# Decoder layer on one core: the second half's projection spread over the whole of the second SSM and finished at its end

## The chip, the cores and the metric

The kernel runs on one core of a Trainium2 chip. The metric is the device time of one execution in microseconds (us); lower is better. Engines are named as the profile names them: PE (TensorE, matrix multiplication; PEld is its loading of weights), DVE (VectorE), ACT (ScalarE), POOL (GpSimd) and SP (SyncE, which here issues nearly all plain transfers). Each engine, and SP's queue, executes its own instructions strictly in the order in which the program lists them.

## The reference, cut to what matters

One layer of a hybrid decoder, on 1024 prompt tokens and 64 sample tokens. A projection of the normalised input gives u (for the SSM), q, k, v (for attention) and two gates; the SSM branch is a complex diagonal recurrence; attention is dilated and windowed; both branches are gated and merged, and a mixture of 16384 single-neuron experts (PEER) follows.

```python
xn = rmsnorm(x, g_mix)
u, q, k, v, ga, gb = split_projection(xn, w_in)
y_ssm, hT_re, hT_im = ssm_branch(u, h0_re, h0_im, ...)     # h[t] = a*h[t-1] + B u[t];  y = Re(C h) + D u
hs = jax.nn.gelu(y_ssm.reshape(B, S, SSM_WIDTH))
branch_a = (hs @ w_glu_a) * sigmoid(hs @ w_glu_b)
...                                                        # dilated attention of q, k, v -> attn
branch_b = attn @ w_attn_proj
x = x + (sigmoid(ga) * branch_a + sigmoid(gb) * branch_b) @ w_out
x = x + peer_ffn(rmsnorm(x, g_ffn), w_qp, sub_keys, u_tab, v_tab)
# peer_ffn: 8 heads x top 16 of 16384 experts per token:
#   act = gelu(xb . u_tab[eidx]);  out = sum(gate * act * v_tab[eidx])
```

## The kernel before, in words

The tokens are worked off in two halves: half 0 has 512 prompt tokens and the 64 samples, half 1 the other 512 prompt tokens. For each half the order is: projection, SSM (`ssm`), attention, GLU, `w_out`, PEER keys. Half 0 fetches its experts' rows one by one (`gather`, half 0 only); half 1 at the end multiplies with all experts (`dense`, from about 2650 us to the end).

Two streams of work run beside the main order, as Python generators: "ahead" is the projection of half 1 (`inputs`, `project_u`, `project`), and "gather" is the fetching of rows of `u_tab` and `v_tab`. The main order calls `tick(us)` with a rough time for what it has just issued; each stream is then advanced until it has given out as much as `us` times its own rate (`pace` sets a rate; for "ahead" it is `FILL[4]` = 1.5 in the second SSM, for "gather" `GO[2]` = 0.7). A row of "gather" counts as `RATE` = 1.9. `drain` advances a stream to its end, without giving anything to the other one.

```python
def tick(self, us):
    if self.inside:
        return
    for name in list(self.sides):
        s = self.sides[name]
        s[2] += us * s[1]
        while s[2] > 0 and name in self.sides:
            c = self.step(name)
            if name == "ahead":
                us += c
```

The list that comes out is then given to a scheduler, which lays the instructions of each engine in an order by a timeline of its own. So numbers in the ticks move instructions on every engine's list.

Names that matter below, with their lines. A *row* is an indirect DMA on POOL (L1558) that fetches 128 rows of `u_tab`, 128x1024 f32, 0.524 MB, into one of `RB` = 8 buffers; a *dot* is the DVE instruction (L1562) that multiplies such a block with the tokens, sums it, and frees the buffer. A *piece* of a weight matrix (0.524 MB) is loaded by SP (L132), cast on ACT to `wH` (L134) and its remainder made on DVE as `wL` (L136); one piece feeds 24 matmuls `mm<-xn.,w.` of 512 columns (two pieces 96 of 256 columns for v).

The second SSM, `ssm(1)`, has three parts. *Loads*: for eight groups q, `uk` and `P` are loaded (L677, L681), transposed and multiplied on PE, and written to the state `X` by ACT (L693). *Scan*: 23 steps on DVE of five instructions each (L711 to L715): 7 of 512 elements, 8 of 64, and 8 of 448, one for each q. *Output*: for each q, `M` and `Q` are loaded (L744, L746), PE does 16 matmuls of each (with `U`, L754, and with `X`), ACT applies Gelu into `Y` (L756), and SP stores `Y` to `hs_scr` (L763). `uk`, `ug`, `P`, `M`, `Q` and `Y` share six buffers, so two q are under way at most.

After the SSM comes attention: `attn_ahead(1)` loads the first q, k and v (L881 to L908), which needs the space that the projection's tiles held; DVE adds the mask (L931), and that writes into space that the SSM's tiles held, `Y` among them. Then DVE combines the three groups and PE transposes `hsn` for the GLU.

Of the kernel before, what the change touches and what calls it, by code (L numbers as in the profile page):

```python
# [37 lines left out]
RATES = (1.0, 1.3, 1.0, 1.0, 0.86, 1.0, 0.6)  # L38
RB = 8
GL = 20  # L40
GO = (2, 0, 0.7)
LEAD = 160

VT = (2, 3)
SSMT = (10.0, 0.0, 5.0)
NS = 2


# [19 lines left out]
class Prog:  # L68
# [231 lines left out]
    def phases(self, es):  # L300
# [21 lines left out]
        self.pace("ahead", FILL[4])  # L322
        self.pace("gather", GO[2])
        self.mark("ssm1")
# [332 lines left out]
    def ssm(self, h):  # L657
        tc, nc, a, s = self.tc, self.nc, self.a, self.scr[h]
        sm = h == 0
        nk = 64 + 8 * sm  # L660
        ng = 8 if h else 16
        v = nc.vector
        with tc.tile_pool(name=f"ssm{h}", bufs=1) as sp:
            U = sp.tile([128, 64, nk], F32, name="U")

            o = 8 * sm
            X = sp.tile([128, 65 + 2 * o, 64], F32, name="X")
            big = lambda nm: sp.tile([128, 128 * ng], F32, name=nm, tag="big", bufs=5 + h)
            if sm:
                nc.sync.dma_start(X[:, 0:8], a["h0"].rearrange("p (b g) -> p b g", b=8))  # L670
                v.memset(X[:, o], 0.0)
            else:
                v.tensor_copy(X[:, o], self.hfin)
            urow = s["u"].rearrange("(k t) c -> k t c", t=8)
            for q in range(64 // ng):
                uk = big("uk")[:nk].rearrange("k (s c) -> k s c", s=8)
                nc.sync.dma_start(uk, urow[:, :, q * 16 * ng:(q + 1) * 16 * ng])  # L677
                ug = big("ug")[:nk].rearrange("k (g s c) -> k g s c", g=ng, s=8)
                nc.scalar.copy(ug, uk[:, ::-1, :].rearrange("k s (g c) -> k g s c", g=ng))
                P = big("P").rearrange("p (g n) -> p g n", g=ng)  # L680
                nc.sync.dma_start(P, self.Pd[:, q * ng:q * ng + ng])  # L681
                for j0 in range(0, ng, 4):
                    ps = self.trt()
                    for j in range(4):
                        nc.tensor.transpose(ps[:, j * nk:(j + 1) * nk], ug[:, j0 + j].rearrange("k s c -> k (s c)"),
                                            self.ident[:nk, :nk])
                    g0 = q * ng + j0
                    nc.scalar.copy(U[:, g0:g0 + 4, :], ps[:, :4 * nk].rearrange("p (g k) -> p g k", g=4))
                    ps = self.trt()
                    pv = ps[:, :4 * nk].rearrange("p (g k) -> p g k", g=4)  # L690
                    for j in range(4):
                        self.mm(pv[:, j, :], P[:, j0 + j, :], U[:, g0 + j, :], start=True, stop=True)
                    nc.scalar.copy(X[:, o + 1:o + 65, g0:g0 + 4].rearrange("p k g -> p g k"), pv[:, :, nk - 64:])  # L693
                    if sm:
                        nc.scalar.copy(X[:, 73:81, g0:g0 + 4].rearrange("p k g -> p g k"), pv[:, :, 0:8])
                self.tick(SSMT[0])

            a8 = sp.tile([128, 8, 2, 64], F32, name="a8")
            nc.sync.dma_start(a8, self.a8)
            lo, hi = slice(0, 64), slice(64, 128)  # L700

            def step(c, p, a, sh):

                n = 64 * sh[1] if len(sh) == 3 else 64 if len(sh) == 2 else 448
                t1, t2 = (sp.tile([128, 512], F32, name="st", tag="st", bufs=2)[:, :n] for _ in range(2))
                if len(sh) == 3:
                    t1, t2 = (t.rearrange("p (x g) -> p x g", g=64) for t in (t1, t2))
                if len(sh) == 4:
                    t1, t2 = (t.rearrange("p (x y g) -> p x y g", x=8, g=8) for t in (t1, t2))
                w = lambda x: x.to_broadcast([x.shape[0]] + sh[1:])  # L710
                v.tensor_mul(t1, w(p), w(a[0]))  # L711
                v.tensor_mul(t2[lo], w(p[hi]), w(a[1][hi]))
                v.tensor_mul(t2[hi], w(p[lo]), w(a[1][lo]))
                v.tensor_add(c, c, t1)
                self.last = v.tensor_add(c, c, t2)  # L715

            if h:
                self.drain("ahead")
                self.es1.close()
                self.attn_ahead(1)  # L720

            xv = X[:, o + 1:o + 65].rearrange("p (j i) g -> p i j g", i=8)
            xb = X[:, o:o + 64].rearrange("p (j i) g -> p j i g", i=8)
            one = [a8[:, 0, x].unsqueeze(1) for x in range(2)]
            for i in range(1, 8):
                step(xv[:, i], xv[:, i - 1], one, [128, 8, 64])
                self.tick(SSMT[1])
            for j in range(8):
                step(X[:, o + 8 * j + 8], X[:, o + 8 * j], [a8[:, 7, x] for x in range(2)], [128, 64])
                self.tick(SSMT[1])  # L730
            for gs in range(0, 64, 8):
                g = slice(gs, gs + 8)
                step(xb[:, :, 1:8, g], xb[:, :, 0:1, g], [a8[:, None, 0:7, x, g] for x in range(2)], [128, 8, 7, 8])
                self.tick(SSMT[1])
            if not sm:
                nc.sync.dma_start(a["ssm_p"], X[:, 64])
            else:
                v.tensor_copy(self.hfin, X[:, 72])
                step(X[:, 73:81], X[:, 0:8], one, [128, 8, 64])
                nc.sync.dma_start(a["ssm_s"], X[:, 73:81])  # L740
            hrow = [self.scr[i]["hs"].rearrange("(k t) c -> k t c", t=8) for i in range(2)]
            for q in range(64 // ng):
                M = big("M").rearrange("p (g x) -> p g x", g=ng)
                nc.sync.dma_start(M, self.Mx[:, q * ng:q * ng + ng, :])  # L744
                Q = big("Q").rearrange("p (g x) -> p g x", g=ng)
                nc.sync.dma_start(Q, self.Qd[:, q * ng:q * ng + ng, :])  # L746
                Y = big("Y")[:nk].rearrange("k (t c) -> k t c", t=8)
                for j0 in range(0, ng, 4):
                    ps = self.mmt() if h else self.trt()
                    pv = ps[:nk].rearrange("k (g x) -> k g x", g=4)  # L750
                    for j in range(4):
                        gl = j0 + j
                        g = q * ng + gl
                        nc.tensor.matmul(pv[:, j, :], lhsT=U[:, g, :], rhs=M[:, gl, :], start=True, stop=False)  # L754
                        self.mm(pv[:, j, :], X[:, :o + 64, g], Q[:, gl, :], start=False, stop=True)
                    nc.scalar.activation(Y[:, :, j0 * 16:j0 * 16 + 64].rearrange("k t (g c) -> k g t c", g=4),  # L756
                                         pv.rearrange("k g (t c) -> k g t c", t=8), AF.Gelu_apprx_tanh)
                cols = slice(q * 16 * ng, (q + 1) * 16 * ng)
                if sm:
                    nc.sync.dma_start(hrow[1][0:8, :, cols], Y[0:8])  # L760
                    nc.sync.dma_start(hrow[0][:, :, cols], Y[8:72])
                else:
                    nc.sync.dma_start(hrow[1][8:72, :, cols], Y)  # L763
                self.tick(SSMT[2])


    def nat(self, x, g, i):
# [464 lines left out]
    def peer_keys(self, h):  # L1232
# [7 lines left out]
        with ExitStack() as es:  # L1240
# [15 lines left out]
            with tc.tile_pool(name=f"pk{h}", bufs=1, side="right") as kp, ExitStack() as eg:  # L1256
# [28 lines left out]
                for i in range(ntl):  # L1285
                    rows = 128 if i < 4 else 64
                    self.choose(kp, h, i, rows, sv[i], si[i], (lambda: self.early(da, x)) if h else None)
                    if h == 0:
                        self.tick(30.0)
                    if h == 0 and i == GO[0]:  # L1290
                        self.beside("gather", self.gather(), GO[1])
                    if h:
# [452 lines left out]
```

## Time and profile before

| | |
|---|---|
| median of 3 runs | 4047.9 us (4040.63 to 4048.96) |
| the profiled execution, its own time | 4032.86 us |
| its span from first to last instruction | 4031.1 us |
| share of the span in which each engine is busy | PE 93%, DVE 73%, ACT 36%, POOL 36% |
| mean granted TensorE clock | 0.961 |
| moved by DMA | 1112.83 MB, 276 GB/s over the span |

The profiled execution is one execution with 1.8 us outside its span. All times on the trace are counted from the span's start.

### The profile page before, as it was taken

How to read it: one execution, taken by the hardware profiler on the slowest of the kernel's cores; microseconds unless marked ns; L12 is line 12 of the kernel's file. 1: busy time of each engine (PE TensorE's matmuls, PEld its weight loads, DVE VectorE, ACT ScalarE, POOL GpSimd, SP SyncE). 2: the span in 40 equal slices, each digit the busy share in tenths (PEclk: the TensorE clock that was granted, in tenths of full speed). 3: DMA queues.
4: the chain of work that ended last, by engine and by line, in shares of the span. 5: the costliest groups of instructions: out<-in, count | busy, mean ns of one | idle time of the engine just before them, and what ended most of it. 6: DMA issues, size and time to landing. Idle time of an engine off the chain costs nothing.

```text
span 4031.1 us, 72558 instructions
## 1 busy us (share of the span) xinstructions
PE 3738.5 (93%) x27907; PEld 3380.1 (84%) x27907; DVE 2943.4 (73%) x6796; ACT 1433.1 (36%) x2756; POOL 1444.1 (36%) x1236
## 2 busy tenths in 40 slices
PE   8889989899989967799979999879999999999997
PEld 8789965589878755597859899769999999999997
DVE  8627233445985767866999977668767999889986
ACT  3232224323234316322216888812222222222222
POOL 1620000000004424445563544433346755545550
PEclk9999989899999978899989999989999999999999
DMA  5574579544369989799897899999989999988993
GB/s 166 158 236 154 194 252 343 181 131 163 99 200 318 321 299 306 264 345 346 300 322 262 294 345 337 339 344 332 329 307 338 362 336 331 323 308 306 324 316 111
DMA packets 448987, 1112.83 MB, mean 276 GB/s; under 512 B 44656, under 2 KB 189424, under 8 KB 443008
## 3 DMA queue, kind: packets, MB, share of 16 engines
q1 hardware_dynamic: 301184, 571.26, 41.8%
q0 software_dynamic: 147456, 536.94, 37.0%
q8 instruction: 219, 3.59, 0.4%
q14 instruction: 128, 1.05, 0.1%
HBM read 991.77 MB, written 124.27 MB: 277 GB/s over the span
## 4 chain that ended last, share of the span: by engine, by line
PE 54%; DVE 6%; DMA 6%; issue 2%; ACT 2%; POOL 0%; SPq 0%; DVEq 0%; ACTq 0%; POOLq 0%
PE mm L80 31%; PE tr L80 20%; PE va L1640 2%; DVE row L1562 2%; DMA row<-in_u_tab,ei 1%; DMA G_scr<-Gt 1%; DMA Q<-Q_scr 1%; DVE wL L136 1%; DMA row<-in_v_tab,eT 1%; DMA V<-v_scr 0%; ACT Gt L1397 0%; DMA kT<-k_scr 0%; ACT sm L936 0%; DVE rest L1306 0%; DMA hs_scr<-Y 0%
## 5 line engine op out<-in xcount | busy, mean ns | idle before, releaser
L1558 POOL DMA_INDIRECT row<-in_u_tab,ei x512 | 664.3, 1297 | 986.7 <-DVE row L1562 451.3
L134 ACT CAST wH<-wraw 128x1024 fp32r<-128x1024 f32 (+1 forms) x476 | 492.3, 1035 | 1245.5 <-PE mm L80 915.5
L136 DVE TENSOR_TENSOR wL<-wraw,wH 128x1024 fp32r<-128x1024 f32 (+1 forms) x476 | 577.7, 1214 | 377.7 <-ACT wH L134 365.0
L1562 DVE SCALAR_TENSOR_TENSOR row<-row,gxn 128x1024 f32<-128x1024 f32 x512 | 616.8, 1217 | 48.4 <-DMA row<-in_u_tab,ei 41.8
L80 PE MATMUL tr<-x2H,wH 128*128 128x288 f32 x2048 | 611.7, 299 | 6.4 <-ACT a L1408 4.6
L80 PE MATMUL tr<-x2L,wH 128*128 128x288 f32 x2048 | 609.3, 297 | 0.0
L80 PE MATMUL tr<-x2H,wL 128*128 128x288 f32 x2048 | 609.1, 297 | 0.0
L80 PE MATMUL mm<-WH,wH 128*128 128x288 f32 (+2 forms) x2048 | 474.0, 295 | 18.6 <-ACT WH L186 18.2
L80 PE MATMUL mm<-WL,wH 128*128 128x288 f32 (+2 forms) x2048 | 473.8, 295 | 0.4 <-DVE WL L187 0.4
L80 PE MATMUL mm<-WH,wL 128*128 128x288 f32 (+2 forms) x2048 | 468.1, 294 | 0.0
L1590 POOL DMA_INDIRECT row<-in_v_tab,ei x256 | 350.9, 1371 | 293.3 <-DVE x3v L1596 240.7
L1624 POOL DMA_INDIRECT row<-in_v_tab,eT x256 | 315.7, 1233 | 386.4 <-DVE row L1562 228.4
L80 PEld LDWEIGHTS tr<-x2H,wH 128*128 128x128 f32 x2048 | 385.1, 188 | 16.3 <-ACT a L1408 7.2
L80 PEld LDWEIGHTS tr<-x2L,wH 128*128 128x128 f32 x2048 | 385.1, 188 | 2.5 <-issue 2.5
L80 PEld LDWEIGHTS tr<-x2H,wL 128*128 128x128 f32 x2048 | 385.0, 188 | 2.5 <-issue 2.5
L80 PEld LDWEIGHTS mm<-WH,wH 128*128 128x128 f32 x2048 | 339.8, 188 | 27.3 <-ACT WH L186 19.9
L80 PEld LDWEIGHTS mm<-WL,wH 128*128 128x128 f32 x2048 | 342.0, 188 | 4.1 <-issue 2.5
L80 PEld LDWEIGHTS mm<-WH,wL 128*128 128x128 f32 x2048 | 339.1, 188 | 1.7 <-issue 1.7
L1596 DVE SCALAR_TENSOR_TENSOR x3v<-row,act,x3v 128x1024 f32<-128x1024 f32 x256 | 327.4, 1279 | 3.0 <-DMA x3v<-x_scr 0.7
L80 PE MATMUL mm<-xnH,wL 128*128 128x288 f32 (+1 forms) x960 | 319.9, 333 | 2.7 <-DVE wL L136 2.7
L80 PE MATMUL mm<-xnH,wH 128*128 128x288 f32 (+1 forms) x960 | 322.3, 336 | 0.0
L80 PE MATMUL mm<-xnL,wH 128*128 128x288 f32 (+1 forms) x960 | 319.2, 332 | 0.0
(392 smaller groups left out, 7760.8 us busy)
## 6 DMA issues: line engine op xcount, KB each, us to landing
wraw<-in_vT SPq DMA_DIRECT2D x132, 512.0 KB
wraw<-in_uT SPq DMA_DIRECT2D x128, 512.0 KB
G_scr<-Gt SPq DMA_DIRECT2D x18, 2048.0 KB
G<-G_scr SPq DMA_DIRECT2D x32, 1152.0 KB
cc<-in_kc SPq DMA_DIRECT2D x48, 512.0 KB
cc<-in_vc SPq DMA_DIRECT2D x48, 512.0 KB
wraw<-in_w_g SPq DMA_DIRECT2D x32, 512.0 KB
wraw<-in_w_qp SPq DMA_DIRECT2D x32, 512.0 KB
```

Of the source, the lines that this page charges most:

```text
L80: self.last = self.nc.tensor.matmul(out, lhsT=lhsT, rhs=rhs, **kw)
L134: nc.scalar.copy(h, raw)
L136: nc.vector.tensor_sub(l, raw, h.bitcast(F32))
L1558: self.after(nc.gpsimd.indirect_dma_start(out=row, out_offset=None, in_=a["u_tab"], in_offset=bass.IndirectOffsetOnAxis(ap=ei[:, k:k + 1], ...
L1562: self.after(v.scalar_tensor_tensor(row, row, 1.0, xn, op0=ALU.mult, op1=ALU.mult, accum_out=act[:, k:k + 1]))
L1590: self.after(nc.gpsimd.indirect_dma_start(out=row, out_offset=None, in_=a["v_tab"], in_offset=bass.IndirectOffsetOnAxis(ap=ei[:, k:k + 1], ...
L1596: self.after(v.scalar_tensor_tensor(x3, row, self.gw[i][:, k:k + 1], x3, op0=ALU.mult, op1=ALU.add))
L1624: self.after(nc.gpsimd.indirect_dma_start(out=row, out_offset=None, in_=a["v_tab"], in_offset=bass.IndirectOffsetOnAxis(ap=eT[:, tk:tk + 1 ...
L1640: self.after(nc.tensor.matmul(va[0][c:c + 32, :], lhsT=self.strips[:, s, j, 31 - t - s:63 - t - s], rhs=rows[s * 2 + j][:, b * 512:(b + 1) ...
```

## The change

The projection of half 1 is no longer drained between the SSM's loads and its scan. The ticks of the second SSM are set apart from those of the first (`SSMT` now has a value for each half): 4.0 instead of 10.0 after each load group, 3.0 instead of 0 after each of the 23 scan steps, 5.0 as before after each output group; so both streams are advanced in the scan, too. From the output on, "gather" has the rate 0.4 instead of 0.7. What is left of the projection is drained after the output, and the first loads of attention are issued there.

```diff
-GO = (2, 0, 0.7)
+GO = (2, 0, 0.7, 0.4)
...
-SSMT = (10.0, 0.0, 5.0)
+SSMT = ((10.0, 4.0), (0.0, 3.0), (5.0, 5.0))
...
-                self.tick(SSMT[0])
+                self.tick(SSMT[0][h])
...
-            if h:
-                self.drain("ahead")
-                self.es1.close()
-                self.attn_ahead(1)
...
-                self.tick(SSMT[1])
+                self.tick(SSMT[1][h])
...
+            if h:
+                self.pace("gather", GO[3])
...
-                self.tick(SSMT[2])
+                self.tick(SSMT[2][h])
+        if h:
+            self.drain("ahead")
+            self.es1.close()
+            self.attn_ahead(1)
```

The lists of all engines are the same up to the second SSM's loads, with the same number of instructions in all. What stands where on DVE, in the scan, before (L1562 is a dot, L136 a piece of weights, L711 to L715 one scan step, here for two of the eight last steps):

```order
L715 TENSOR_TENSOR X<-X,st 128x8x7x8
L711 TENSOR_TENSOR st<-X,a_13984 128x448
L1562 SCALAR_TENSOR_TENSOR row,act<-row,gxn 128x1024 x2
L712 TENSOR_TENSOR st<-X,a_13984 64x448
L713 TENSOR_TENSOR st<-X,a_13984 64x448
L714 TENSOR_TENSOR X<-X,st 128x8x7x8
L715 TENSOR_TENSOR X<-X,st 128x8x7x8
L711 TENSOR_TENSOR st<-X,a_13984 128x448
```

And now, at the same place (a dot is L1564 here, since two lines were added):

```order
L715 TENSOR_TENSOR X<-X,st 128x8x7x8
L711 TENSOR_TENSOR st<-X,a_13376 128x448
L1564 SCALAR_TENSOR_TENSOR row,act<-row,gxn 128x1024 x2
L712 TENSOR_TENSOR st<-X,a_13376 64x448
L713 TENSOR_TENSOR st<-X,a_13376 64x448
L714 TENSOR_TENSOR X<-X,st 128x8x7x8
L136 TENSOR_TENSOR wL<-wraw,wH 128x1024
L1564 SCALAR_TENSOR_TENSOR row,act<-row,gxn 128x1024 x2
L715 TENSOR_TENSOR X<-X,st 128x8x7x8
L711 TENSOR_TENSOR st<-X,a_13376 128x448
L1564 SCALAR_TENSOR_TENSOR row,act<-row,gxn 128x1024
L136 TENSOR_TENSOR wL<-wraw,wH 128x1024
```

A scan step now has two to four dots and a piece of weights between its five instructions where it had none to two dots.

On DVE at the end of the scan, before (L931 is attention's first mask):

```order
L715 TENSOR_TENSOR X<-X,st 128x8x7x8
L1562 SCALAR_TENSOR_TENSOR row,act<-row,gxn 128x1024 x14
L931 ISA sm,stat<-mm,mask_69 128x256
```

And now (L933 is that mask's line now):

```order
L715 TENSOR_TENSOR X<-X,st 128x8x7x8
L1564 SCALAR_TENSOR_TENSOR row,act<-row,gxn 128x1024 x2
L136 TENSOR_TENSOR wL<-wraw,wH 128x1024
L1564 SCALAR_TENSOR_TENSOR row,act<-row,gxn 128x1024 x5
L136 TENSOR_TENSOR wL<-wraw,wH 128x1024
L1564 SCALAR_TENSOR_TENSOR row,act<-row,gxn 128x1024 x3
L136 TENSOR_TENSOR wL<-wraw,wH 128x512
L1564 SCALAR_TENSOR_TENSOR row,act<-row,gxn 128x1024 x12
L815 MEMSET stat 128x384 x2
L1564 SCALAR_TENSOR_TENSOR row,act<-row,gxn 128x1024 x6
L933 ISA sm,stat<-mm,mask_69 128x256
```

28 dots and three pieces of weights of the GLU stand between the scan and attention, where 14 dots stood.

On SP, at the output's second group of M and Q, before:

```order
L621 DMA sg_scr_140<-qo 128x512
L744 DMA M<-Mx_scr 128x1024
L746 DMA Q<-Q_scr 128x1024
L881 DMA q<-q_scr_137 128x1024
L888 DMA V<-v_scr_139 128x4x256
L897 DMA kT<-k_scr_138 128x2x512
L907 DMA V<-v_scr_133 128x256
L908 DMA kT<-k_scr_132 128x2x128
L763 DMA hs_scr_141<-Y 512x1x128
```

And now:

```order
L742 DMA M<-Mx_scr 128x1024
L744 DMA Q<-Q_scr 128x1024
L621 DMA sg_scr_140<-qo 128x512
L132 DMA wraw<-in_w_g 128x1024
L761 DMA hs_scr_141<-Y 512x1x128
L621 DMA sg_scr_140<-qo 128x512
L132 DMA wraw<-in_w_g 128x1024
L132 DMA wraw<-in_w_b 128x1024
L621 DMA sg_scr_140<-qo 128x512
L742 DMA M<-Mx_scr 128x1024
```

The loads of attention have left this place (they now stand after the sixth group's M and Q), and the last pieces of the projection's weights stand between the groups instead.

## Rows read from the trace of the kernel before

**Rows 1.** The page's head: span and number of instructions.

```profile
span 4031.1 us, 72558 instructions
```

**Rows 2.** Windows: stretch, length, busy us of PE, PEld, DVE, ACT, POOL, clock, DMA share, GB/s.

```profile
1200.00:1240.00 40.00, 33.78 (x165) 27.26 (x164) 10.79 (x15) 19.94 (x29) 4.60 (x3) 0.91 0.79 224
1240.00:1363.00 123.00, 118.08 (x682) 100.54 (x681) 73.23 (x109) 45.80 (x70) 60.99 (x47) 1.00 0.97 349
1363.00:1465.00 102.00, 80.52 (x361) 64.19 (x360) 98.96 (x178) 26.46 (x36) 32.82 (x25) 0.90 0.88 307
1468.00:1500.00 32.00, 19.56 (x115) 18.25 (x113) 12.86 (x22) 4.73 (x8) 17.02 (x13) 0.71 0.97 357
1465.00:1515.00 50.00, 34.94 (x208) 32.34 (x208) 16.04 (x29) 7.10 (x12) 18.98 (x14) 0.74 0.79 279
1515.00:1640.00 125.00, 98.63 (x893) 68.21 (x893) 94.20 (x324) 88.09 (x277) 60.64 (x48) 0.87 0.89 291
1640.00:1680.00 40.00, 21.87 (x74) 12.66 (x75) 37.75 (x75) 6.14 (x14) 17.32 (x15) 0.74 0.82 288
2700.00:4000.00 1300.00, 1299.58 (x9823) 1272.07 (x9822) 1103.05 (x1595) 349.94 (x490) 641.45 (x484) 1.00 0.88 315
```

**Rows 3.** The chain that ended last, end of the loads: start, us, what.

```profile
1339.87 9.80 PE mm L80 x42
...
1363.48 0.69 DVE st L711
```

**Rows 4.** DVE's groups by shape, 1363 to 1465 us: busy us, mean ns, idle before.

```profile
L1562 DVE SCALAR_TENSOR_TENSOR row<-row,gxn 128x1024 f32<-128x1024 f32 x24 | 28.7, 1218 | 0.1
L136 DVE TENSOR_TENSOR wL<-wraw,wH 128x1024 fp32r<-128x1024 f32 x13 | 15.8, 1219 | 0.1
L714 DVE TENSOR_TENSOR X<-X,st 128x448 f32<-128x448 f32 x8 | 5.0, 624 | 0.2
...
L714 DVE TENSOR_TENSOR X<-X,st 128x512 f32<-128x512 f32 x7 | 4.8, 686 | 0.0
...
L714 DVE TENSOR_TENSOR X<-X,st 128x64 f32<-128x64 f32 x8 | 1.8, 225 | 0.2
```

**Rows 5.** DVE's timeline, end of the scan to attention's first mask.

```profile
1463.69 0.62 DVE L715 TENSOR_TENSOR X<-X,st 128x448 f32<-128x448 f32 x1
...
1514.82 0.42 DVE L931 CUSTOM_DVE_ANT_0 sm<-mm,mask 128x256 f32<-128x256 f32 x1 [29.44 <-DMA hs_scr<-Y]
```

**Rows 6.** The chain that ended last, in the output: start, us, what.

```profile
1454.15 10.64 DMA Q<-Q_scr
1464.93 0.66 PE mm L80 x2
...
1472.60 8.57 DMA Q<-Q_scr
1481.31 0.66 PE mm L80 x2
...
1511.26 3.10 DMA hs_scr<-Y
```

**Rows 7.** Who waited for whom, 1228 to 1363 us: total us, times, longest.

```profile
POOL row L1558 <- DVE row L1562: 149.3, 17, 89.4
```

**Rows 8.** The same, 1465 to 1520 us.

```profile
POOL row L1558 <- DVE stat L933: 31.1, 1, 31.1
...
DVE row L1562 <- DMA row<-in_u_tab,ei: 4.5, 3, 3.4
```

**Rows 9.** Windows of line L1558 alone: stretch, length, POOL busy us (rows issued), clock, DMA.

```profile
1228.00:1363.00 135.00, 65.03 (x50) 1.00 0.95 340
1363.00:1410.00 47.00, 25.20 (x19) 1.00 0.91 310
...
1465.00:1515.00 50.00, 18.98 (x14) 0.74 0.79 279
```

**Rows 10.** DVE's groups by shape, 1640 to 1680 us.

```profile
L1562 DVE SCALAR_TENSOR_TENSOR row<-row,gxn 128x1024 f32<-128x1024 f32 x19 | 22.9, 1214 | 0.0
```

## What is expected, and how it is worked out

> **What bounds the kernel now.** I began with the windows. From 2700 to 4000 us PE is busy for 1299.58 of 1300 us at full clock [rows 2]: there PE is the bound, nothing before it is caught up later, and whatever the second SSM gains or loses arrives at the end of the span undiminished. The change acts between 1200 and 1680 us, and there the bound changes hands. In the loads, 1240 to 1363 us, PE is busy 118 of 123 us and DMA's share is 0.97 [rows 2]; PE works mostly on the projection. The scan, 1363 to 1465 us, is DVE's: 98.96 of 102 us [rows 2]. In the output, 1465 to 1515 us, nobody is busy: PE 34.94 of 50 us at a clock of 0.74 (between the levels 1.2 and 2.4 GHz), DVE 16.04 [rows 2]. The chain shows why: a Q load of 10.64 us, matmuls at 1464.93, another Q load, matmuls at 1481.31, and so on to the last store of `Y` at 1511.26 [rows 6]. Six buffers let two groups be under way, so loads come in bursts of two. DVE stands 29.44 us and begins attention at 1514.82, when that last store has landed [rows 5]: the mask writes where `Y` was. After attention, 1640 to 1680 us, DVE is busy 37.75 of 40 us [rows 2], and 19 dots, 22.9 us, are over half of that [rows 10].
>
> So the idle time is in the output; the projection's tail ran ahead of it, beside the scan.
>
> **The change, part by part.**
>
> *The loads end earlier.* I counted the lists. From the first transpose of `uk` to the last product with `P`, PE's list had 428 matmuls of the projection with 512 columns, and has 152; the 192 of 256 columns, and all 128 of the SSM are as before. A projection matmul takes 9.80 us / 42 = 0.233 us [rows 3]; 276 x 0.233 = 64 us, and 16 transposes of `kn` less give 1 or 2 more. The scan then starts at 1363.5 [rows 3] - 65 = 1298 us. This holds if PE's stalls stay as they are; they were 6.2 + 4.9 us [rows 2], and closer loads can double them: 1290 to 1310.
>
> *The scan gets longer.* Its own work is 7 x 5 x 0.686 + 8 x 5 x 0.225 + 8 x 5 x 0.624 = 58 us [rows 4]. The list put 23 dots and 14 pieces of `wL` between its instructions, and puts 55 and 21. Dots follow each other at 1.145 us (the next instruction starts before the accumulator is read), pieces take 1.219 [rows 4]. Check on before: 58 + 26.3 + 17.1 = 101; measured 1363.5 to 1464.3 = 101 [rows 3, 5]. Now: + 32 x 1.145 + 7 x 1.219 = 45, so 146 us, and the scan ends at 1444 instead of 1464. No gain in DVE's work, only its start moved.
>
> *The output.* In the lists 48 of its 256 matmuls (three of eight groups) now stand among the projection's last ones, and PE has 442 of the projection's 512-column matmuls, 103 us, from scan's start to the first output group; DVE finishes the first group's step after 16 of its 23 steps, 34 dots and 13 pieces: 36 + 39 + 16 = 91 us. So PE does not wait there, and three groups' M and Q land under the projection, which ends near 1444 as well. After that five groups remain. Before, the seven groups after 1464 took until 1511, 6.6 us each [rows 6]; five take 33 us, the store 3.1 [rows 6], so 1481. The first loads of attention, which used to go out before 1452, now stand between the groups: two sets of 1.8 MB (q, V and kT of 0.52 each, and 0.13 each of the first half's V and kT), 10 us at the rate of 357 GB/s [rows 2]. By the engines attention starts at 1481 to 1491.
>
> *The bytes.* Attention also waits for the dots that stand ahead of its first mask: 106 instead of 88. At 1515 us all eight buffers were full as well (POOL waited 31.1 us for DVE [rows 8]), 96 rows; now 106 to 110 must have come, 10 to 14 more, 6.3 MB at 0.524. Moved from 1200 to 1515 us: 224 x 40 + 349 x 123 + 307 x 102 + 279 x 50 = 97.2 MB [rows 2]. With 6.3 more, and 9.0 of it by 1240 as before, 94.5 MB are left. At a share of 0.97 DMA moved 349 and 357 GB/s [rows 2], 360 and 368 at a full share; at 364, 94.5 MB take 260 us, until 1500. At 349 it is 1511.
>
> The Trainium skill bears on this (DMA: Bandwidth & Descriptors, sections Issuing engines are not separate DMA queues, and Where 436 GB/s comes from): transfers started from several engines share the same 16 DMA engines and gain only issue time, and between HBM and SBUF the memory's side, about 358 GB/s per core, binds. It speaks against this change, since POOL's rows and SP's M and Q then divide one rate. By that page's figure attention starts, as an estimate, near 1504, by the engines' sum alone at 1481 to 1491; the rows at a share of 0.97 agree with the page.
>
> I take 1500, the byte sum: -15 us, bounds -34 (1481) and -4 (1511).
>
> *Attention* gets 47 dots instead of 40: 7 x 1.22 = +8.5 us if DVE sets its pace, nothing if not. DVE is busy 94 of 125 us and DMA's share is 0.89 [rows 2]; I take +6. The boundary between the first two token tiles, where new tokens `gxn` are loaded and eight dots wait for them, moves from attention's end to its middle; I price it within that.
>
> *Combining.* Between attention's last mask and the GLU's first instruction stand 14 dots instead of 30. Sixteen less are 18 us at 1.145, but PE must still transpose `hsn` and `hs_scr` must be loaded, PE being busy 21.87 us there at a clock of 0.74 [rows 2]. I take -13, bounds -18 and -5.
>
> *Later.* From there to `dense` 186 dots instead of 188, and beside `dense` seven rows of `u_tab` and eight of `v_tab` fewer, where PE is the bound: 0. The rate 0.4 is in these counts. The drain's work is covered by the wait for M and Q; without that cover it would cost what stands after the third group, 28 matmuls, 6.5 us.
>
> Sum: -15 + 6 - 13 = -22. On the profiled execution, 4032.9 us (the span of 4031.1 [rows 1] and 1.8 around it), that is 4011; that execution was 15 us faster than the median 4047.9, below all three timed ones. On the median I forecast 4047.9 - 22 = 4026 us.
>
> **The rivals.**
>
> *Rows come too slowly: slower.* After the scan's start 83 dots stand ahead of attention; with eight rows in the buffers 75 must be fetched. Attention and combining together give 7 us back, so it breaks even at 1514.8 + 7 = 1522 us: 75 rows in 224 us, 0.335 a microsecond. Below that DVE, which keeps its order, stands in the scan before dots whose rows have not come, and the output waits behind it. Measured: 50 in 135 us (0.37), 19 in 47 (0.40), but 14 in 50 (0.28) in the output [rows 9]. At 0.28, 75 rows take 268 us: attention at 1566, +51 - 7 = +44, 4092 us; at 0.32, 4058. For it: DMA is at 0.97 while rows, M and Q come together [rows 2]. Against it: POOL stood 149.3 us for buffers that DVE had not freed, longer than any other wait there [rows 7], and DVE waited only 4.5 us for rows in the output [rows 8], so 0.28 was not transport's limit.
>
> *The time is given back: same.* The bytes pass at 349 GB/s (1511, -4), attention pays its 8.5 us in full, and combining gains only 5 because `hsn` binds: about 0, 4048. For it: shares near 0.9 all through [rows 2], DVE's dots being moved and not removed. Against it: the 29 us in which DVE stands [rows 5] are now filled.
>
> *The engines' sum holds: faster still.* DMA passes more than the 364 GB/s taken, attention starts at 1481 without paying: -34 + 0 - 18 = -52, 3996. This is the near end of the forecast's own range, not a case apart.
>
> **How the numbers follow.** No change that is smaller than 0.2% (8 us) can be told from none here. The forecast (faster by 8 to 52 us, 3996 to 4040) gets 0.66, nothing 0.18, slower 0.16. The predicted time is the forecast's, 4026. The range 4000 to 4052 leaves out the forecast's last 4 us and the larger part of the slow rival, about 2 in 10. Faster 0.66, same 0.18, slower 0.16.
>
> **What would show it.** In the new trace: the first scan step (L711) near 1298 and the last (L715) near 1444, DVE busy throughout; three Gelus of `Y` pairs before the projection's last matmul; the first mask near 1500, its wait far under 29 us and ended by a row or by the last store; DMA share from 1240 to 1500 near 0.97; combining shorter by about 13 us; `dense` of the same length. Waits of DVE for rows (L1564 on `row`) of 20 us or more in the scan would speak for the slow rival. I am wrong if the loads do not come earlier (PE stalling for `uk` and `P`), or if later stages lie otherwise by more than 10 us through the scheduler's new order, which I priced at nothing.

## The result, and the profile after

The changed kernel takes 4075.2 us (median of 4 runs, 4068.18 to 4081.91), the kernel before 4046.1 us beside it (4 runs): a ratio of 1.0073, 95% interval 1.0055 to 1.0091. It is 29 us slower, where 4026 us was forecast. The profiled execution took 4068.18 us, of which its span, against that of [rows 1]:

```profile
span 4066.5 us, 72554 instructions
```

The windows from the loads to the first mask; columns as in [rows 2].

```profile
1240.00:1295.00 55.00, 55.00 (x396) 50.27 (x395) 27.98 (x42) 24.57 (x42) 22.23 (x17) 1.00 0.96 328
...
1295.00:1446.00 151.00, 141.05 (x614) 112.41 (x613) 141.07 (x246) 44.14 (x56) 72.14 (x55) 0.95 0.92 327
1446.00:1520.00 74.00, 31.24 (x166) 26.87 (x165) 37.12 (x62) 8.37 (x14) 40.20 (x29) 0.72 1.01 384
1240.00:1520.00 280.00, 227.29 (x1173) 189.55 (x1172) 206.18 (x348) 77.08 (x111) 134.56 (x100) 0.90 0.95 342
...
1520.00:1534.00 14.00, 11.51 (x78) 10.20 (x77) 0.09 (x1) 2.37 (x4) 0.00 (x0) 0.87 0.21 45
```

In the third window neither PE nor DVE is busy for much more than half of the time, while the DMA engines are full. DVE's timeline shows the same stretch (start, us, instruction; in brackets the idle time before it and its end): the scan's first step, its last, the last dot ahead of attention, the first mask.

```profile
1294.61 0.69 DVE L711 TENSOR_TENSOR st<-X,a 128x512 f32<-128x512 f32 x1 [0.18 <-ACT X L693]
...
1445.70 0.62 DVE L715 TENSOR_TENSOR X<-X,st 128x448 f32<-128x448 f32 x1
...
1497.16 1.22 DVE L1564 SCALAR_TENSOR_TENSOR row<-row,gxn 128x1024 f32<-128x1024 f32 x1
...
1533.91 0.42 DVE L933 CUSTOM_DVE_ANT_0 sm<-mm,mask 128x256 f32<-128x256 f32 x1 [35.52 <-DMA hs_scr<-Y]
```

DVE still stands for the store of `Y`, 35.5 us instead of 29.4 [rows 5], and from 1533.9 instead of 1514.8 on. Who waited for whom, 1440 to 1535 us:

```profile
PE mm L752 <- DMA M<-Mx_scr: 38.4, 4, 17.7
DVE sm L933 <- DMA hs_scr<-Y: 35.5, 1, 35.5
...
DVE row L1564 <- DMA row<-in_u_tab,ei: 9.1, 12, 2.1
```

PE stands for `M`; DVE hardly for rows. SP's queue shows the longest of these waits, that for the seventh `M`:

```profile
1473.77 0.32 SPq L621 DMA_DIRECT2D sg_scr<-qo  x1
1474.19 0.38 SPq L742 DMA_DIRECT2D M<-Mx_scr  x1
1474.66 0.39 SPq L744 DMA_DIRECT2D Q<-Q_scr  x1
1490.62 0.32 SPq L883 DMA_DIRECT2D q<-q_scr  x1
...
1500.04 3.18 SPq L883 DMA_DIRECT2D q<-q_scr  x1
...
1508.59 0.44 SPq L910 DMA_DIRECT2D kT<-k_scr  x1
1511.16 0.33 SPq L742 DMA_DIRECT2D M<-Mx_scr  x1
```

Attention's first load stands until the projection's last store (1473.77) has landed, and ten loads go out before the next `M` is asked for. What the DMA engines did meanwhile, 1465 to 1500 us (packets, MB, share of the 16 engines; POOL's rows are the software queue, everything SP issues the hardware queue):

```profile
DMA packets 5213, 14.34 MB, mean 410 GB/s; under 512 B 482, under 2 KB 1594, under 8 KB 5209
...
q0 software_dynamic: 2500, 9.10, 64.2%
q1 hardware_dynamic: 2709, 5.20, 38.9%
```

Rows took 64% of them. The loss does not end there. The table has starts in us from two traces of each kernel (the second ones are the runs c_before and c_after below, from another job). Its first row is an instruction ahead of the second SSM's loads, the last on DVE's list (its 2240th) up to which all kernels of this document agree:

```profile
1218.45 1.23 DVE L136 TENSOR_TENSOR wL<-wraw,wH 128x1024 fp32r<-128x1024 f32 x1 [10.87 <-ACT wH L134]
```

Here it is from the kernel after. It starts at 1216.2 us in the first trace of the kernel before and between 1215.9 and 1226.0 in the other traces, so clock times of two traces differ by up to 10 us before the change can act. Where that matters, a time below is *counted from the common start*, which means that this instruction's start is taken off; in this count the scan's first step comes at 76.0 to 76.2 us in eleven of the twelve traces with the change and at 77.7 in c_after.

| | before | c_before | after | c_after |
|---|---|---|---|---|
| common start | 1216.2 | 1218.4 | 1218.5 | 1222.1 |
| last Gelu of `Y` | 1510.7 | 1513.2 | 1529.7 | 1534.5 |
| first mask | 1514.8 | 1517.4 | 1533.9 | 1538.7 |
| last mask | 1620.5 | 1618.1 | 1644.1 | 1646.6 |
| last product of the GLU | 1820.4 | 1823.8 | 1835.5 | 1838.3 |
| first product of the PEER keys | 1898.4 | 1905.5 | 1924.7 | 1926.1 |
| first mask, counted from the common start | 298.6 | 299.0 | 315.5 | 316.6 |
| last product of the GLU, so counted | 604.1 | 605.4 | 617.1 | 616.2 |
| span | 4031.1 | 4046.1 | 4066.5 | 4083.3 |
| from the GLU's last product to the end | 2210.7 | 2222.3 | 2230.9 | 2245.0 |

Counted from the common start, the first mask is 17 to 18 us late, and by the GLU's end 11 to 13 us are lost. Behind it 20 and 23 more are lost, in stages that the prediction priced at nothing. Of these, 6 to 8 us lie between `w_out` and the keys, where PE's timeline has this row in the kernel after, and nothing of the kind in the kernel before:

```profile
1914.32 3.64 PE L1642 MATMUL va<-row,strips 128*32 128x512 f32 x16 [5.79 <-DMA row<-in_v_tab,eT]
```

Products of the row stream with rows of `v_tab` now stand in PE's list between the norm's transposes, and PE waits for their row.

### The profile page after: what moved, and what is told of

It reads as the page before. It is cut to its first block, busy times and chain, and to the rows that moved or that the text cites. A ratio compares the mean times of both kernels' runs of the same rounds, so it can differ in the third digit from the quotient of the medians.

```text
span 4066.5 us, 72554 instructions
## 1 busy us (share of the span) xinstructions
PE 3745.4 (92%) x27907; PEld 3388.8 (83%) x27907; DVE 2943.3 (72%) x6796; ACT 1438.4 (35%) x2756; POOL 1416.7 (35%) x1236
## 5 line engine op out<-in xcount | busy, mean ns | idle before, releaser
L1560 POOL DMA_INDIRECT row<-in_u_tab,ei x512 | 630.0, 1231 | 945.1 <-DVE row L1564 415.5
L136 DVE TENSOR_TENSOR wL<-wraw,wH 128x1024 fp32r<-128x1024 f32 (+1 forms) x476 | 577.3, 1213 | 380.4 <-ACT wH L134 363.7
L1564 DVE SCALAR_TENSOR_TENSOR row<-row,gxn 128x1024 f32<-128x1024 f32 x512 | 619.4, 1220 | 62.6 <-DMA row<-in_u_tab,ei 39.5
L80 PEld LDWEIGHTS tr<-x2H,wH 128*128 128x128 f32 x2048 | 387.3, 189 | 23.8 <-ACT a L1410 12.4
```

Of the source, the lines that this page charges most:

```text
L80: self.last = self.nc.tensor.matmul(out, lhsT=lhsT, rhs=rhs, **kw)
L136: nc.vector.tensor_sub(l, raw, h.bitcast(F32))
L1560: self.after(nc.gpsimd.indirect_dma_start(out=row, out_offset=None, in_=a["u_tab"], in_offset=bass.IndirectOffsetOnAxis(ap=ei[:, k:k + 1], ...
L1564: self.after(v.scalar_tensor_tensor(row, row, 1.0, xn, op0=ALU.mult, op1=ALU.mult, accum_out=act[:, k:k + 1]))
```

## The experiments

Each ratio is taken against runs of the kernel before on the same chip, in the same job.

**Why attention starts late.** Four kernels, each the kernel after with an edit. The first puts attention's loads behind the last `Q` in SP's list (an ordering without a wait):

```diff
+def ld(self, dst, src):
+    inst = self.nc.sync.dma_start(dst, src)
+    if self.behind:
+        self.tc.add_manual_dep(inst.ins, self.lastq.ins.name, ...)
...
+            self.behind = True
             self.attn_ahead(1)
+            self.behind = False
```

> The kernel after, with attention's first loads (q, V, kT) given out behind the last load of Q on SP instead of ahead of the last two groups' M and Q; rows and ticks as in the kernel after. Theory S (SP's order): M and Q of the last two groups no longer stand 15.5 us for the projection's last store and 20 us while ten loads are issued; group six is asked for near 1492 instead of 1511 us, the first mask comes near 1516 instead of 1534, and the time is about 18 us under the kernel after. Theory B (bytes): the 16 DMA engines are full from 1440 to 1520 us anyway; only the 3.6 MB of attention's loads move behind, 9 us at 400 GB/s: first mask near 1525, and then attention's first product waits for them. Theory L (later lists): at most half of the loss lies here; from the end of the GLU to the end the kernel still loses about 20 us against the kernel before, whatever the first mask does, so the time stays over the kernel before.

Measured: ratio 1.0014 (1.0002 to 1.0026). The common start and the last Gelu in this trace:

```profile
1226.00 1.23 DVE L137 TENSOR_TENSOR wL<-wraw,wH 128x1024 fp32r<-128x1024 f32 x1 [11.10 <-PE tr L81]
...
1521.28 0.59 ACT L755 ACTIVATE Y<-mm 64x512 f32<-64x512 f32 x1 [0.89 <-PE mm L81]
```

Counted from the common start the last Gelu comes at 295.3 instead of 311.3, 16.0 us earlier (by the clock it is 8.5, since this trace began the second SSM 7.5 us later). That is nearer to theory S's 18 than to theory B's 9. The bytes explain 9 of them: from the scan's end to 5 us before the last Gelu 25.1 MB moved instead of 28.6, at 388 GB/s. The rest goes with the loads' place: SP asks for the seventh `M` at 1495.4 instead of 1511.2 us, 23 us earlier counted from the common start, and the last two groups' `M` no longer land together behind everything else. The first mask came at 1531.4, only 10 us earlier in this count, since the last store of `Y` now stood behind the ten loads (10.1 us from Gelu to mask instead of 4.2). The time fell by 24 us by the ratios, of which 11 lie before the GLU's end (1832.1).

```diff
-GO = (2, 0, 0.7, 0.4)
+GO = (2, 0, 0.7, 0.0)
```

> The kernel after with gather's rate 0.0 instead of 0.4 in the output: 14 dots fewer ahead of the first mask (92 instead of 106). Attention's loads still stand ahead of the last groups' M and Q, now of three. Theory S: the first mask stays within 8 us of 1534, since SP still stands for the projection's last store. Theory B: 14 rows are 7.3 MB, 18 us at 400 GB/s: first mask near 1516. Theory L: the phase of the row stream changes by 8 to 14 rows in the later stages, and the time from the end of the GLU to the end changes by 10 us or more either way.

Measured: 1.0022 (1.0009 to 1.0036); last Gelu 1517.1, first mask 1521.2, 17.8 us earlier counted from the common start (1223.5). Theory B's 18 is met, and theory S, which allowed 8, fails as it was put. But the run does not part the two: without the rows SP's loads were issued faster too, and the seventh `M` was asked for at 1497.9, 18 us earlier in this count.

```diff
             if h:
+                self.drain("ahead")
+                self.es1.close()
+                self.attn_ahead(1)
                 self.pace("gather", GO[3])
...
-        if h:
-            self.drain("ahead")
-            self.es1.close()
-            self.attn_ahead(1)
```

> The kernel after with the drain, the release of the projection's space and attention's loads put between the scan and the output instead of behind the output; the ticks in loads and scan stay, so the projection is spread beside the scan, and attention's loads stand ahead of five groups, as before the change. Theory S: an early block on SP is as bad or worse than a late one, unless the projection's last store has landed by then; SP's stand for that store shows before the third group's loads, first mask at 1525 to 1545. Theory B: nothing of the bytes changes except the order; first mask near 1530. If the first mask comes before 1515 it was the late place of attention's loads that cost the time.

Measured: 1.0091 (1.0068 to 1.0113); first mask 1541.5. With attention's loads ahead of the whole output it comes 5.5 us later still, counted from the common start, so putting them back to their old place is no cure.

The fourth has the edits of the first and the second.

> Both the first and the second edit: attention's loads behind the last Q, and gather's rate 0.0 in the output (91 dots ahead of the first mask). Theory S: first mask near 1510, little better than with the first edit alone. Theory B: 3.6 + 7.3 MB leave the way of M and Q, 27 us at 400 GB/s: first mask near 1505, which is where the prediction's sum by engines and bytes put it. Theory L: the time from the end of the GLU to the end is what decides between faster and slower than the kernel before; with a first mask at 1505 and a loss of 20 us later, the time is 4050 to 4060.

Measured: 1.0010 (0.9993 to 1.0027). Last Gelu 1504.0, 28.5 us earlier than in the kernel after counted from the common start (1221.3), where B gave 27 for 10.9 MB and S 24. The mask stands behind the held-up store again:

```profile
1514.12 0.42 DVE L941 CUSTOM_DVE_ANT_0 sm<-mm,mask 128x256 f32<-128x256 f32 x1 [30.64 <-DMA hs_scr<-Y]
```

So what passes ahead of the last `M` and `Q` sets the output's end: 3.6, 7.3 and 10.9 MB less gave 16.0, 17.8 and 28.5 us, where the bytes alone come to 9, 18 and 27 at 400 GB/s. For the rows bytes are enough; for attention's loads SP's order counts as well. No run takes away SP's stand and leaves the bytes, so its share is not shown by itself. In the last of these kernels the GLU ends at 596.9 in the same count, 7 to 9 us ahead of the kernel before, and its time is still not lower: what is gained by then is lost behind the GLU, where it takes 2236.5 us.

**Two traces more.** Both kernels unchanged.

> The kernel before, unchanged: a second trace of it, since the profiled execution of before was 15 us under the median. Theory N (spread of executions): the stages up to the first mask agree within 5 us with the first trace (1514.8), and the stretch from the end of the GLU to the end is 10 to 20 us longer than its 2211 us. Theory L (the changed kernel's later lists cost 20 us): that stretch is again 2211 us within 5, and an early stage is what was fast.

> The kernel after, unchanged: a second trace. Its first mask is again at 1534 within 5 us, and the end of the GLU at 1836 within 5 if the cause of the loss is in the order of the bytes. From the end of the GLU to the end it took 2231 us in the first trace; theory N: 2225 to 2245, as much as a typical execution of before plus at most 10; theory L: 15 us or more over that of before in the same job.

Measured: 4047.9 and 4085.0 us, one run each; the table above has their stages. Theory N holds for the size of the spread (the stretch behind the GLU is 12 and 14 us longer than in the first traces) and L for the difference: 20.2 us in one pair, 22.7 in the other.

**Rows put off.** The kernel after with gather's rate 0.0 in the scan, and the kernel after without ticks in the scan.

```diff
+            if h:
+                self.pace("gather", 0.0)
             for i in range(1, 8):
```

> The kernel after with gather's rate 0.0 in the scan (and 0.4 in the output, as there): the projection alone is spread beside the scan; 45 dots instead of 106 ahead of the first mask, 163 instead of 198 by the end of the GLU. Theory B (bytes): 61 rows are 32 MB, so the DMA engines no longer bind; the scan is 50 dots or 57 us shorter on DVE (end near 1390), the projection on PE ends near 1415 and the output behind it near 1460: first mask 1455 to 1480. Theory G (the rows are only put off): the rows that are missing come back at 1.22 us of DVE each between the top 16 and the dense stage, where DVE is busy 223 of 237 us; 25 rows against the kernel before are 30 us, so the time is within 15 us of the kernel before although attention starts 40 us earlier. If the rows find room beside the dense stage, where DVE is busy 1103 of 1300 us, the time falls by 20 us or more against the kernel before.

```diff
-SSMT = ((10.0, 4.0), (0.0, 3.0), (5.0, 5.0))
+SSMT = ((10.0, 4.0), (0.0, 0.0), (5.0, 5.0))
```

> The kernel after with 0.0 instead of 3.0 after each scan step: neither stream is advanced in the scan; the second SSM runs almost by itself, and what is left of the projection is drained behind it, so attention waits for the projection. 32 dots at the scan's end, 50 ahead of the first mask, 167 by the end of the GLU. Theory B: the scan ends near 1375, the output near 1420, and the rest of the projection, of which PE had 103 us from the scan's start on, bounds attention's start: near 1480. Theory G as for the other: time within 15 us of the kernel before; else 20 us or more under it.

Measured: 1.0062 (1.0041 to 1.0084) and 1.0123 (1.0099 to 1.0148). Theory B's first masks are missed in both. In the second the projection ended at 1516.3 and the first mask came at 1530.4, not near 1480. In the first the scan ended at 1379.3, but the first mask came at 1513.5, not 1455 to 1480: with the DMA engines free, PE was the bound, and the projection ended at 1456.9, with five output groups behind it. Windows of that kernel, 1380 to 1460 us and the last 50 us:

```profile
1380.00:1460.00 80.00, 80.00 (x402) 65.40 (x401) 26.69 (x33) 23.53 (x32) 12.11 (x9) 1.00 0.65 211
...
4025.00:4075.00 50.00, 3.50 (x31) 3.27 (x30) 42.70 (x118) 3.45 (x6) 18.07 (x14) 0.56 0.69 245
```

The GLU ended at 1801.0, 24 to 25 us before that of the kernel before counted from the common start (1221.0), and all of it was lost again: PE is busy 3.5 of the last 50 us, where DVE and POOL finish the rows that were put off. In the kernel before POOL issues no row in its last 100 us. Theory G's sign is right, its size is not: 24 us gained by the GLU's end and 25 lost in all make about 49 us for 25 rows, more than DVE's 1.22 us each. What makes them dearer was not taken apart.

**Why the later stages lose.** Gather's rates alone, in the kernel after in the GLU and in the kernel before in attention.

```diff
-RATES = (1.0, 1.3, 1.0, 1.0, 0.86, 1.0, 0.6)
+RATES = (1.0, 0.9, 1.0, 1.0, 0.86, 1.0, 0.6)
```

> The kernel after with gather's rate in the GLU 0.9 instead of 1.3: up to the GLU nothing changes, and from there on the row stream stands as in the kernel before (210 dots at the first top 16, 265 at the first product of gates, 346 at the dense stage, as there; the kernel after has 220, 274, 353). Theory P (phase of the row stream): the loss behind the GLU comes from where the row stream's products with v rows and its change of token tiles fall; the stretch from the GLU's last matmul to the end, 2231 and 2245 us in two traces of the kernel after and 2211 and 2222 in two of the kernel before, comes back to 2210 to 2225, and the time falls by about 20 us against the kernel after, to some 15 us over the kernel before. Rival (order in general): the schedule of those stages is different for some other reason, the stretch stays at 2230 to 2245 and the time within 8 us of the kernel after.

Measured: 1.0012 (0.9998 to 1.0026). First mask 1537.4, as in the kernel after counted from the common start (315.2 for 315.5). The GLU's end, 1833.3, is 6 us earlier in this count, with 37 dots instead of 44 between the last mask and it. The stretch behind it is 2213.5, in the forecast 2210 to 2225. The products of `v_tab` are gone from between the norm's transposes: `w_out`'s last product and the first of the keys in PE's timeline.

```profile
1898.67 0.28 PE L80 MATMUL mm<-wH,mixL 128*128 128x256 f32 x1
...
1909.25 0.61 PE L80 MATMUL mm<-x2H,wH 128*128 128x288 f32 x1
```

10.6 us, where the kernel after needs 17.3.

```diff
-RATES = (1.0, 1.3, 1.0, 1.0, 0.86, 1.0, 0.6)
+RATES = (1.3, 1.3, 1.0, 1.0, 0.86, 1.0, 0.6)
```

> The kernel before with gather's rate in attention 1.3 instead of 1.0: the second SSM is untouched, and the row stream stands at the GLU's end as in the kernel after (198 dots instead of 188, and 222 at the first top 16). Theory P: the first mask stays at 1515 to 1518 us, the stretch from the GLU's end to the end grows by 15 to 25 us against the kernel before, and the time is 15 to 25 us over it, with nothing of the change in it. Rival: the stretch does not grow, and rows done earlier take 10 dots, 12 us of DVE, off the later stages; the time is the same or lower.

Measured: 1.0062 (1.0045 to 1.0079), 25 us more without any edit to the SSM. But most of it lies elsewhere than forecast: counted from the common start the GLU's end moves from 604.1 and 605.4 to 618.2, as attention, with 51 dots instead of 40, takes 117.6 us instead of 105.7 and 100.7. The stretch behind it takes 2214.9, no more than in the kernel before, although products of `v_tab` stand between the transposes here too. This run tells that ten rows taken early are not free; in it theory P fails for the stretch.

```diff
-RATES = (1.0, 1.3, 1.0, 1.0, 0.86, 1.0, 0.6)
+RATES = (1.0, 1.3, 1.0, 1.0, 0.86, 1.3, 0.6)
```

> The kernel before with gather's rate in w_out 1.3 instead of 1.0: no list differs up to the end of the GLU, 188 dots there as before; then 212 instead of 210 at the first top 16, 269 instead of 265 at the product of gates, 350 instead of 346 at the dense stage, nearly as in the two kernels without rows in the output (213, 268, 349), whose stretch behind the GLU took 2236 us. Theory P: the first mask and the GLU's end stay (1515 to 1518, 1820 to 1824), the stretch takes 2225 to 2240 instead of 2211 to 2222, and the time is 8 to 25 us over the kernel before, from two to four rows standing elsewhere. Rival: two to four rows do nothing; the time is within 8 us, and the later loss of the kernel after comes from its early part in some other way.

Measured: 1.0011 (0.9998 to 1.0025). First mask 1522.5, 301.0 counted from the common start (2 us later than before); stretch 2224.4, just short of theory P's 2225 to 2240. By the time the rival holds: two to four rows do little.

**Versions to beat both.** The first is the kernel after with the edits of e5_both, the second set of attention's loads behind the last store of `Y`, and 1.2 as the GLU's rate. The second is the kernel before with gather's rate 0.0 in the output and 1.2 in attention. The last two have gather's rates 0.0 and 1.6, and 0.2 and 1.2, in scan and output of the kernel after, with the loads placed as in the first.

> The kernel after with everything mended that the runs so far put a price on: attention's first loads behind the last Q, the second ones behind the last store of Y, no rows given out in the output, and gather's rate in the GLU 1.2, so that the row stream stands from the GLU on as in the kernel before (211, 265, 346). Theories B and P together: last Gelu near 1504 as with both edits, the store now at once behind it, first mask near 1508; behind the GLU as the kernel before; time 5 to 12 us under the kernel before. If the spread projection is itself the loss, the first mask is not before 1514, and the time is at or over the kernel before.

> The kernel before with gather's rate 0.0 in the second SSM's output, and 1.2 instead of 1.0 in attention, so that the row stream stands from the GLU on as in the kernel before (188, 210, 265, 346). 74 dots instead of 88 ahead of the first mask: 7.3 MB less of rows beside M and Q. Theory B: the DMA engines are at 0.97 there, so M and Q come up to 18 us earlier, first mask 1500 to 1505; attention takes the dots back at 1.22 us each as far as DVE sets its pace (14 dots, 17 us at most); time 0 to 15 us under the kernel before. If rows are not what M and Q wait for, the first mask stays at 1515 and the time is 0 to 10 us over it.

> The projection is spread beside the scan as in the kernel after; gather's rate is 0.0 in the scan and 1.6 in the output, so 57 dots stand between the scan's end and the first mask instead of 28, and the row stream stands from the GLU on nearly as in the kernel before (187, 210, 265, 345); attention's loads stand behind the last Q. Theories B and P: with the projection alone in the scan, the DMA engines moved 211 GB/s from 1380 to 1460 us while PE was the bound there; against 400 GB/s that is room for 15 MB or 28 rows, and DVE is idle two thirds of it. Rows put there cost little: scan's end near 1380, projection's end near 1457, last Gelu 1500 to 1510, end of the GLU at 1805 to 1820, then 2211 to 2222 us: 4018 to 4042 us in all, faster than both kernels by 8 us or more against the kernel before. Rival: the 12 rows for which there is no room come beside the last groups' M and Q, last Gelu at 1515 to 1525, and the time is that of the kernel before within 8 us.

> As the one before it, with gather's rate 0.2 in the scan and 1.2 in the output: 15 more dots in the scan (43 at its end), 46 behind it, 89 ahead of the first mask, 188 at the end of the GLU, 212 at the top 16. Theory B: rows for which there is no room behind the scan find it in the scan (175 GB/s moved from 1300 to 1380 with the projection alone): last Gelu 1500 to 1510, as in the run before it or up to 10 us earlier. Theory P: with 212 and 266 instead of 210 and 265 the row stream stands off its place, and the stretch behind the GLU's end takes up to 2236 us instead of 2211 to 2222.

Measured, in this order: 1.0006 (0.9988 to 1.0023), 1.0016 (1.0004 to 1.0029), 1.0089 (1.0063 to 1.0115), 1.0055 (1.0031 to 1.0079). None beats the kernel before. In e9_all_mended the store is free again (last Gelu 1508.7, first mask 1512.8, 288.9 counted from the common start, 10 us ahead of the kernel before), but attention takes 119.7 us and the GLU ends at 1830.1, 606.2 in this count, 1 to 2 us behind it. Its dots are not the reason, as 45 stand there and the kernel after has 47 in 110.2 us; DVE waited in attention 23.8 us for products of PE, and 12.4 there. What held PE up was not followed. So the two repairs do not add up: 1.0010 (e5_both) and 1.0012 (e7_after_rephased) each for itself, 1.0006 together. In e10_before_fewer_rows the first mask comes at 1510.9, 288.1 and so 10 to 11 us earlier in this count, which is theory B's forecast; the GLU's end is at 605.7, where it was: the 14 dots come back. In e11_rows_behind_scan the room that PE's bound left was hardly used: 18 rows were issued from 1380 to 1460, and 33 from 1460 to 1515, beside the last `M` and `Q`, at a DMA share of 1.03; DVE was through with its dots only at 1525.9, and the mask came at 1532.8. The last Gelu was where the forecast had it, 1509.2; the time is missed by the forecast and by its rival. In e12_rows_spread the last Gelu comes as in e11_rows_behind_scan (292.8 and 293.3 counted from the common start), as forecast, and the first mask at 302.9 instead of 316.9; the stretch of 2224.8 us is inside its bound.

## Why the prediction was wrong

*The loads end earlier*: right; 1294.6 (second trace 1299.8) for 1298.

*The scan gets longer*: right; it ends at 1445.7 for 1444, 151 us for 146.

*The output*: this is the first step that failed, by 34 us (first mask 1533.9 for 1500; 2.2 of them lie ahead of the second SSM). By engines: the first output group came at 1411.2, where 1401 follows from my 103 us, and the projection's last product at 1457.2; that it ends "near 1444" had no sum of its own behind it, and PE was already busy 141 of 151 us in the scan. Behind it five groups took 72.5 us to the last Gelu, where I summed 33. That 33 rested on a miscount: the Gelus of `Y` in the kernel before show two groups done by 1450 and six, not seven, behind the scan, 7.8 us each, so five would have been 39. Attention's loads, 10 us in this sum, cost 16 (e1). By bytes: the sum was nearly right, 342 GB/s x 280 us = 95.8 MB by 1520 for 94.5 forecast, but the rate was 342 and not 364, with shares of 0.96 and 0.92 in the first two windows: 16 to 20 us. And I took the last bytes to be a row's, behind which attention starts at once. They were those of the last `M` and `Q`; behind them stand their products, Gelu and store, 14 us. e1, e2 and e5 show it: whatever passes later lets the output end earlier. SP's queue had no term in my sum: it stood for the projection's last store and then for ten issues, 36 us from the sixth `Q` to the seventh `M`, and e1 shows that this order costs more than the loads' bytes. The wait under 29 us that I named as a mark became 35.5.

The slow rival had the right sign and the wrong place. It has DVE stand in the scan for rows; DVE waited 9.1 us for rows in all, 2.1 at the longest, and 29 rows were issued in 74 us (0.39 a microsecond, above the 0.335 at which it breaks even). Rows came fast enough; it was `M` and `Q` that they, and attention's loads, displaced.

*Attention*: right; 110.2 us from first to last mask instead of 105.7, +4.5 (second traces +7) for +6.

*Combining*: right in size; from the last mask to the GLU's last product 191.5 us instead of 199.9, -8.4 (second traces -14), for -13.

*Later*: this is the second step that failed: +20 us for 0, through the mark that I had named last, later stages lying otherwise by more than 10 us. I had counted dots and not looked at where they stand in PE's list. That the row stream is what costs most of this in the kernel after is shown by e7_after_rephased: the same kernel up to attention's end, ten rows fewer at the first top 16, the stretch back at 2213.5 and the time 25 us lower by the ratios. Whether it is the number of rows or where the lists put them, this run does not tell. In all 17 traces the time from `w_out`'s last product to the first of the keys went with one thing: 9.7 to 11.1 us in the seven whose list has only transposes there (the kernel before twice, e7, e9, e10, e12, e13), 13.9 to 18.5 us in the ten with products of `v_tab` between them. These products were not moved by themselves, and they do not decide the whole stretch: e8 has them and took 2214.9 us, e12 and e13 have not and took 2224.8 and 2224.4; two traces of one kernel are 12 and 14 us apart. Two things stay open: the other 12 to 17 us of the loss, of which 12 and 14 lie between the first product of the keys and PE's last longer gap ahead of the dense stage; and why e1_loads_behind, with the row stream's counts of the kernel after, lost less behind the GLU (2225.8). Every one of these kernels has its later lists laid anew, and the stretch took 2211 to 2247 us in those that finish their rows in time.

The dense stage, last, is right: from the end of PE's last longer gap (2695.0, before 2656.3) to the end 1371.5 us, before 1374.8.

Parts of the loss and its sum in the profiled pair: +2.2 ahead of the second SSM, which is not the change's, +16.9 from there to the first mask, +4.5 in attention, -8.4 up to the GLU's end, +20.2 behind it: 35.4 us, the difference of the spans.

## What to carry to other kernels

A stream of row fetches that is hidden by count still takes its share of the transfers: when the loads that the main order waits for must pass beside it, price what moves ahead of the last needed byte, and the work behind that byte. Where a scheduler lays all lists anew, a moved tick is a change to every later stage; look in each waiting engine's list for products whose operand comes by DMA, and count how many rows are left at the end, where nothing hides them. To tell what an edit did inside a long trace, count from an instruction that both lists have ahead of it: here clock times alone made an effect of 16 us look like 8.5, which hid that the order on SP's queue counts.

## What the runs showed of the hardware

The 16 DMA engines moved more than the sum had allowed: 410 GB/s from 1465 to 1500 us, 391 from 1450 to 1500. The Trainium skill (HBM Reference, Specifications (TRN2)) says that a core streaming alone goes well above its share of about 358 GB/s, to about 425; the trace agrees, and the figure that the prediction drew from another page of it, 358, is not this kernel's limit.

From 1465 to 1500 us, with the DMA engines full, packets came nearly in equal numbers from the two queues, 2500 of rows and 2709 of everything that SP issues, but 9.10 and 5.20 MB, as a row's packets were 3.6 KB and the others 1.9 KB on average. So it is in e11_rows_behind_scan from 1460 to 1515 us, 4226 and 4008 packets with 15.39 and 7.12 MB. The Trainium skill (DMA: Bandwidth & Descriptors, Queues, rings and completion order) says that each engine goes round its queues packet by packet; the counts agree, if the profile counts the same packets. SP's loads, in the smaller packets, got 36% and 32% of the bytes beside the rows.
